# Gate and up of a feed-forward layer: six pairs of k-tiles by seven products instead of three, and the sums of weights on GpSimd instead of VectorE

## The chip, the core and the metric

The kernel runs on one core of a Trainium2 chip. The metric is the device time of one execution in microseconds (us), the median of several runs. Five engines work side by side, each on its own queue of instructions, in the order of that queue: TensorE (PE in the rows, with PEld for its weight loads), VectorE (DVE), ScalarE (ACT), GpSimd (POOL) and SyncE (SP, which here only issues the loads from HBM). An instruction that needs another engine's result waits on a semaphore, and everything behind it on its own queue waits with it.

## The reference

Two transformer blocks over 256 tokens of width 2048, in float32. The change touches the last part of the second block, the feed-forward layer with 5632 hidden columns:

```python
h = rmsnorm(x, ffn_norm_w[l])
x = x + (jax.nn.silu(h @ w_gate[l]) * (h @ w_up[l])) @ w_down[l]
```

`w_gate` and `w_up` are 2048 x 5632 and `w_down` is 5632 x 2048. Everything before this (projections, two recurrences, attention) stays as it is.

## The kernel before

All weights stream from HBM. A piece of weights is one tile of 128 partitions x 1024 float32 (`wr`, 5 buffers), loaded by SP. Since TensorE is fed with a shorter format than float32, each piece is cut in two (`cut`, lines 295 to 315): ScalarE casts it to `wh` (line 312), VectorE subtracts that from the piece and writes the rest to `wl` (line 314). `wh` and `wl` have 5 buffers each. A product of one k-tile is then three matmuls, high by high, high by low and low by high (line 219).

The hidden columns of gate and up are taken in 11 blocks of 512. Blocks 0 to 3, 4 to 7 and 8 to 10 make three parts, and behind each part comes its share of the product with `w_down`. In a block the 16 k-tiles of 128 go in 8 pairs. The tokens are two tiles of 128 (t = 0 and 1), so a pair is two blocks of a 2 x 2 product for gate and two for up. There are two plans for a pair (class `Pair`):

- the plain plan, pieces X (gate) and Y (up): eight products, 24 matmuls of 128x512;
- the plan by seven products, pieces A, E, B and C, a form of Winograd's algorithm: 21 matmuls. It needs sums of weights: `w3` (two halves, lines 305 and 306) and `w4` (two halves, lines 307 and 308), each half one subtraction of 128x512 by VectorE. `w3` takes a `wr` buffer and `w4` one of the 23 general pages (`pg`). A (the gate pair, 1024 wide), E (half of the up pair, 512 wide), B (`w3`, 1024) and C (`w4`, 1024) are then cut as other pieces are. It also needs sums of the activations, made once in `operand3` (names `s1` to `s4`, line 1420 on) and kept in a page for each pair; a plain pair needs a difference (`d`) instead.

`SPAIRS = (1, 3, 5)` says which pairs go by seven products. Three of the seven accumulators are in the PSUM pool of the side work (`ps`), and `ff_mid` (lines 1469 to 1476) empties them behind the last such pair. `ff_done` (line 1478 on) empties the others behind the block, computes silu by tanh, multiplies gate by up, transposes and splits the result for `w_down`.

The order on each queue is made by a scheduler that works from the program's order: loads are asked for 5 pieces ahead (`AHEAD`), pieces are cut up to 4 ahead of their products (`CUT`), and side work (`ff_done` of the block before, for one) is put between.

Of the kernel before, what the change touches and what calls it, by code (L numbers as in the profile page):

```python
# [12 lines left out]
F32R = mybir.dt.float32r  # L13
AF = mybir.ActivationFunctionType
ALU = mybir.AluOpType
# [4 lines left out]
P = 128  # L20
# [7 lines left out]
CV = 2  # L28
# [3 lines left out]
CUT = 4  # L32
WB = 5
AHEAD = 5
SPAIRS = (1, 3, 5)
PARTS = ((0, 4), (4, 8), (8, 11))
WN = 1024
WU = 14
# [119 lines left out]
def kernel(ctx, tc, a, out, dbg=None):  # L158
    nc = tc.nc
    PE, V, A, G, SP = nc.tensor, nc.vector, nc.scalar, nc.gpsimd, nc.sync  # L160
# [3 lines left out]
    pg = ctx.enter_context(tc.tile_pool(name="pg", bufs=PGB))  # L164
# [10 lines left out]
    def nm(s):  # L175
        uid[0] += 1
        return f"{s}{uid[0]}"

    def page(dt=F32, n=1024):
        return pg.tile([P, 1088], dt, tag="pg", name=nm("pg"))[:, :n]  # L180

    def half():
        return hp_.tile([P, 512], F32, tag="hp", name=nm("hp"))
# [4 lines left out]
    def bank():  # L188
        return ps.tile([P, 512], F32, tag="sp", name=nm("sp"))
# [4 lines left out]
    def v3(t, b):  # L194
        return t.rearrange("p (a b) -> p a b", b=b)
# [19 lines left out]
    def act(o, x, f, **kw):  # L215
        return A.activation(out=o, in_=x, func=f, **kw)  # L216
# [18 lines left out]
    def tr(o, x):  # L235
        n = x.shape[0]
        PE.transpose(o, x, ident[:n, :n])  # L237
# [18 lines left out]
    def add(ch):  # L256
        ci = len(chunks)
        chunks.append(ch)
        if ch.kind == "pair":
            pieces.extend((ch, k, n, c) for k, n, c in ch.parts)  # L260
            return ci
        m = -(-ch.nk // ch.per)
        k = 0
        sizes = [(ch.nk * (i + 1)) // m - (ch.nk * i) // m for i in range(m)]
        if ci == 0:
            sizes = FIRST
        for n in sizes:
            pieces.append((ch, k, n, None))
            k += n
        return ci  # L270
# [24 lines left out]
    def cut(i):  # L295
        if i >= len(pieces) or i in split:
            return
        ch, k, n, part = pieces[i]
        w = raw.pop(i)
        if part == "A":  # L300

            w2 = raw[i + 1]
            w3 = raw[i + 2] = wp.tile([P, WN], F32, tag="wr", name=nm("wr"), bufs=RB)
            w4 = raw[i + 3] = page()
            V.tensor_tensor(out=w3[:, :512], in0=w2[:, :512], in1=w[:, :512], op=ALU.subtract)  # L305
            V.tensor_tensor(out=w3[:, 512:], in0=w2[:, :512], in1=w2[:, 512:], op=ALU.subtract)  # L306
            V.tensor_tensor(out=w4[:, :512], in0=w2[:, 512:], in1=w3[:, :512], op=ALU.subtract)
            V.tensor_tensor(out=w4[:, 512:], in0=w[:, 512:], in1=w4[:, :512], op=ALU.subtract)  # L308
        x = w[:, 512:] if part == "E" else w[:, :n * ch.width if part is None else 1024]
        sz = x.shape[1]  # L310
        h = wp.tile([P, WN], F32R, tag="wh", name=nm("wh"), bufs=WB)
        A.copy(out=h[:, :sz], in_=x)  # L312
        l = wp.tile([P, WN], F32R, tag="wl", name=nm("wl"), bufs=WB)
        V.tensor_tensor(out=l[:, :sz], in0=x, in1=h[:, :sz].bitcast(F32), op=ALU.subtract)  # L314
        split[i] = (v3(h[:, :sz], ch.width), v3(l[:, :sz], ch.width))
# [70 lines left out]
    def run_stream():  # L386
# [4 lines left out]
        while i < len(pieces):  # L391
# [5 lines left out]
            for j in range(CUT):  # L397
                cut(i + j)
# [68 lines left out]
    def vec(row):  # L467
        return vt[:, row:row + 1]
# [931 lines left out]
    dform = []  # L1400

    def operand3(nat, n, hi, lo):

        f = v3(page(), S)
        for j in (0, 2):
            b = bank()
            b3 = v3(b, S)
            for q in range(2):
                for t in range(2):
                    tr(b3[:, q, t * P:(t + 1) * P], nat[:, t, (j + q) * P:(j + q + 1) * P])  # L1410
            yield
            for q in range(2):
                act(f[:, j + q, :], b3[:, q, :], AF.Copy, scale=vec(V_FN + 4 * n + j + q))
            k = slice(4 * n + j, 4 * n + j + 2)
            A.copy(out=hi[:, k, :], in_=f[:, j:j + 2, :])
            V.tensor_tensor(out=lo[:, k, :], in0=f[:, j:j + 2, :], in1=hi[:, k, :].bitcast(F32), op=ALU.subtract)
            yield
            p = 2 * n + j // 2
            x = half()
            if p in SPAIRS:  # L1420
                a11, a21, a12, a22 = (f[:, j + q, t * P:(t + 1) * P] for q in range(2) for t in range(2))
                s1, s3, s2, s4 = (x[:, q * P:(q + 1) * P] for q in range(4))
                V.tensor_tensor(out=s1, in0=a21, in1=a22, op=ALU.add)
                V.tensor_tensor(out=s3, in0=a21, in1=a11, op=ALU.subtract)
                V.tensor_tensor(out=s2, in0=s1, in1=a11, op=ALU.subtract)
                V.tensor_tensor(out=s4, in0=a12, in1=s2, op=ALU.subtract)
                h, w, c = page(F32R), 512, 0
                names = [(nme, 2 * p) for nme in ("s1", "s3", "s2", "s4")]
            else:
                V.tensor_tensor(out=v3(x[:, :S], P), in0=f[:, j:j + 2, 0:P], in1=f[:, j:j + 2, P:S], op=ALU.subtract)  # L1430
                if not dform or dform[-1][1] == 512:
                    dform.append([pg.tile([P, 1024], F32R, tag="cv", name=nm("cv"), bufs=CV) if len(dform) < CV else page(F32R), 0])
                h, c = dform[-1]
                w = S
                dform[-1][1] += S
                names = [("d", 2 * p), ("d", 2 * p + 1)]
            A.copy(out=h[:, c:c + w], in_=x[:, :w])
            V.tensor_tensor(out=h[:, 512 + c:512 + c + w], in0=x[:, :w], in1=h[:, c:c + w].bitcast(F32), op=ALU.subtract)
            for q, nme in enumerate(names):
                op3.forms[nme] = (h[:, c + q * P:c + (q + 1) * P], h[:, 512 + c + q * P:512 + c + (q + 1) * P])  # L1440
            for q in range(2):
                op3.t[4 * n + j + q] = (hi, lo, 4 * n + j + q)
                op3.cols[4 * n + j + q] = 1
            yield
# [24 lines left out]
    def ff_mid(po, st):  # L1469

        x, v = page(), page()
        A.copy(out=x[:, :512], in_=po["1"])
        V.tensor_tensor(out=x[:, 512:], in0=x[:, :512], in1=po["6"], op=ALU.add)
        V.tensor_tensor(out=v[:, :512], in0=x[:, 512:], in1=po["7"], op=ALU.add)
        st["x"], st["v"] = x, v
        yield

    def ff_done(po, st, part, k0):

        x, v = st["x"], st["v"]  # L1480
        lo_, hi_ = slice(0, 512), slice(512, 1024)
        g = page()
        V.tensor_tensor(out=g[:, lo_], in0=x[:, lo_], in1=po["2"], op=ALU.add)  # L1483
        V.tensor_tensor(out=g[:, hi_], in0=v[:, lo_], in1=po["4"], op=ALU.add)
        V.tensor_tensor(out=v[:, hi_], in0=x[:, hi_], in1=po["5"], op=ALU.add)
        V.tensor_tensor(out=v[:, lo_], in0=v[:, lo_], in1=po["5"], op=ALU.add)
        V.tensor_tensor(out=v[:, hi_], in0=v[:, hi_], in1=po["3"], op=ALU.add)
        for t, c in ((0, lo_), (1, hi_)):
            act(x[:, c], g[:, c], AF.Tanh, scale=r3h[:, t:t + 1])
        yield  # L1490
        stt(g, x, 1.0, g, ALU.add, ALU.mult)
        mul(g[:, lo_], g[:, lo_], v[:, hi_])
        mul(g[:, hi_], g[:, hi_], v[:, lo_])
        yield
        u = v3(g, 512)
        hi, lo = page(F32R), page(F32R)
        for j in (0, 2):
            b = bank()
            b3 = v3(b, S)
            for q in range(2):  # L1500
                for t in range(2):
                    tr(b3[:, q, t * P:(t + 1) * P], u[:, t, (j + q) * P:(j + q + 1) * P])
            yield
            c = slice(j * S, (j + 2) * S)
            A.copy(out=hi[:, c], in_=b)
            V.tensor_tensor(out=lo[:, c], in0=b, in1=hi[:, c].bitcast(F32), op=ALU.subtract)
            for q in range(j, j + 2):
                opf[part].t[k0 + q] = (v3(hi, S), v3(lo, S), q)
                opf[part].cols[k0 + q] = 1
            yield  # L1510
# [39 lines left out]
    w2 = a["w_in_2"].rearrange("o k n -> (o k) n")  # L1550
# [56 lines left out]
    for n in range(4):  # L1607
        st = {}
        c = slice(n * 512, (n + 1) * 512)
# [22 lines left out]
    for part, (b0, b1) in enumerate(PARTS):  # L1632
        for blk in range(b0, b1):
            st = {}
            c = slice(blk * 512, (blk + 1) * 512)
            add(Pair(wg[:, c], wu[:, c], 16, op3, SPAIRS, lambda po, st=st: ff_mid(po, st),
                     lambda po, st=st, part=part, blk=blk: ff_done(po, st, part, 4 * blk)))
# [28 lines left out]
```

## Time and profile before

| | us |
|---|---|
| median of 3 runs | 2319.6 |
| lowest, highest | 2319.56, 2323.78 |
| the profiled execution, whole | 2321.56 |
| its span in the trace | 2319.7 |
| TensorE busy | 2302.9 (99%) |
| VectorE busy | 1594.3 (69%) |
| ScalarE busy | 1155.2 (50%) |
| GpSimd busy | 91.3 (4%) |

The span is the time from the first to the last instruction of the profiled execution. Busy time is the time in which an engine had an instruction under way; consecutive instructions of one engine overlap a little, so the distance between two starts is shorter than a duration. The feed-forward layer runs from about 1580 us to the end.

### The profile page before, as it was taken

The page shows a single profiled execution, that of the slowest core. Times are in us where ns is not written, and L with a number is a line of the kernel's source. Part 1 is how long each engine was busy: PE and PEld are TensorE (multiplying, and loading weights), DVE is VectorE, ACT ScalarE, POOL GpSimd, SP SyncE. Part 2 cuts the span into 40 slices and gives each one's busy share as a digit, 9 for nine tenths or more (in the row PEclk, how much of TensorE's full clock was granted, in tenths as well). Part 3 has the DMA queues.
Part 4 walks back from the last instruction along what each step waited for, and adds up shares of the span by engine and source line. Part 5 has one row for each costly group of instructions (what it writes and reads, how often), then busy time and mean ns, then how long its engine had stood idle before and what let it go on. Part 6 is the DMA issues. An engine that isn't in the chain of part 4 may idle for free.

```text
span 2319.7 us, 29508 instructions
## 1 busy us (share of the span) xinstructions
PE 2302.9 (99%) x11101; PEld 1899.4 (82%) x11101; DVE 1594.3 (69%) x2164; ACT 1155.2 (50%) x1521; POOL 91.3 (4%) x122
## 2 busy tenths in 40 slices
PE   8999999999999999999999999999999999999998
PEld 7888888888888888888888777888878888888886
DVE  6777678785676655455555566667897588856985
ACT  5553444544454444444444455456555355544553
POOL 0112001000100000000010000000000000000000
PEclk9999999999999999999999999999999999999999
DMA  7667545666555666666676554455657556665664
GB/s 245 184 182 211 167 137 173 178 203 183 168 163 158 187 185 196 203 201 203 187 211 182 162 148 140 145 185 161 222 176 227 175 184 203 222 196 170 204 217 137
DMA packets 225198, 427.97 MB, mean 184 GB/s; under 512 B 20200, under 2 KB 20624, under 8 KB 225056
## 3 DMA queue, kind: packets, MB, share of 16 engines
q1 hardware_dynamic: 219136, 411.08, 58.2%
q0 software_dynamic: 5056, 13.70, 2.1%
q8 instruction: 87, 1.43, 0.3%
q10 hardware_dynamic: 864, 1.31, 0.2%
q14 instruction: 55, 0.45, 0.1%
HBM read 422.31 MB, written 3.73 MB: 184 GB/s over the span
## 4 chain that ended last, share of the span: by engine, by line
PE 97%; DMA 1%; DVE 1%; issue 0%; ACT 0%; SPq 0%; POOLq 0%; POOL 0%; DVEq 0%; ACTq 0%
PE mm L219 89%; PE sp L219 4%; PE sp L237 3%; DMA wr<-in_w_up_dram 1%; PE sp L797 1%; PE sp L1227 0%; DMA wr<-in_w_in_dram 0%; DVE wl L314 0%; ACT wh L312 0%; SPq L248 0%; SPq L288 0%; DVE wr L306 0%; DVE wr L305 0%; ACT pg L216 0%; DVE pg L1483 0%
## 5 line engine op out<-in xcount | busy, mean ns | idle before, releaser
L219 PE MATMUL mm<-wh,hl 128*128 128x512 f32 x4186 | 1337.3, 394 | 2.4 <-ACT wh L312 1.4
L314 DVE TENSOR_TENSOR wl<-wr,wh 128x1024 fp32r<-128x1024 f32 (+2 forms) x811 | 966.5, 1200 | 518.3 <-ACT wh L312 514.9
L312 ACT CAST wh<-wr 128x1024 fp32r<-128x1024 f32 (+2 forms) x811 | 831.5, 1033 | 893.8 <-PE mm L219 806.5
L219 PEld LDWEIGHTS mm<-wh,hl 128*128 128x128 f32 x4186 | 784.0, 188 | 168.6 <-issue 5.8
L219 PE MATMUL mm<-wl,hl 128*128 128x512 f32 x2093 | 819.3, 392 | 0.6 <-DVE wl L314 0.6
L219 PE MATMUL mm<-wh,pg 128*128 128x512 f32 x1780 | 565.2, 391 | 0.0
L219 PEld LDWEIGHTS mm<-wl,hl 128*128 128x128 f32 x2093 | 393.7, 188 | 80.9 <-DVE wl L314 1.8
L219 PEld LDWEIGHTS mm<-wh,pg 128*128 128x128 f32 x1780 | 333.7, 188 | 69.7 <-issue 0.9
L219 PE MATMUL mm<-wl,pg 128*128 128x512 f32 x890 | 346.6, 389 | 0.0
L219 PEld LDWEIGHTS mm<-wl,pg 128*128 128x128 f32 x890 | 167.1, 188 | 34.4
L237 PE MATMUL sp<-con,pg 128*128 128x128 f32 x555 | 85.8, 275 | 5.2 <-DMA pg<-in_consts_dram 4.9
L237 PEld LDWEIGHTS sp<-con,pg 128*128 128x128 f32 x555 | 68.1, 141 | 21.8 <-issue 7.0
L312 ACT CAST wh<-pg 128x1024 fp32r<-128x1024 f32 x33 | 34.7, 1053 | 82.6 <-DVE pg L308 54.6
L213 DVE SCALAR_TENSOR_TENSOR pg<-cv,vt,pg 128x255 f32<-128x255 f32 (+2 forms) x144 | 61.6, 478 | 1.3 <-ACT pg L216 1.2
L219 PE MATMUL mm<-wh,cv 128*128 128x512 f32 x176 | 61.5, 390 | 0.0
L314 DVE TENSOR_TENSOR wl<-pg,wh 128x1024 fp32r<-128x1024 f32 x33 | 40.4, 1224 | 22.8 <-ACT wh L312 22.8
L219 PE MATMUL sp<-pg,pg 128*128 128x128 f32 (+3 forms) x320 | 50.2, 315 | 0.0
L219 PEld LDWEIGHTS sp<-pg,pg 128*128 128x128 f32 (+1 forms) x320 | 42.8, 190 | 6.1 <-issue 2.9
L216 ACT ACTIVATE pg<-sp,vt 128x256 fp32r<-128x256 f32 (+1 forms) x64 | 28.4, 471 | 28.5 <-PE sp L237 17.2
L219 PEld LDWEIGHTS mm<-wh,cv 128*128 128x128 f32 x176 | 33.0, 188 | 6.7
L216 ACT ACTIVATE pg<-pg 128x512 f32<-128x512 f32 (+2 forms) x54 | 35.3, 674 | 6.2 <-DVE pg L890 3.1
L305 DVE TENSOR_TENSOR wr<-wr,wr 128x512 f32<-128x512 f32 x33 | 22.8, 691 | 21.5 <-DMA wr<-in_w_up_dram 21.4
(273 smaller groups left out, 1190.3 us busy)
## 6 DMA issues: line engine op xcount, KB each, us to landing
wr<-in_w_in_dram SPq DMA_DIRECT2D x416, 512.0 KB, 3.8
wr<-in_w_out_dram SPq DMA_DIRECT2D x96, 512.0 KB, 4.5
wr<-in_w_gate_dram SPq DMA_DIRECT2D x88, 512.0 KB, 3.9
wr<-in_w_up_dram SPq DMA_DIRECT2D x88, 512.0 KB, 4.6
wr<-in_w_down_dram SPq DMA_DIRECT2D x88, 512.0 KB, 4.7
pg<-zsc POOLq DMA_DIRECT2D x8, 384.0 KB, 4.6
pg<-in_x_dram SPq DMA_DIRECT2D x4, 512.0 KB, 6.0
pg<-gsc POOLq DMA_DIRECT2D x4, 512.0 KB, 6.3
```

Of the source, the lines that this page charges most:

```text
L213: return V.scalar_tensor_tensor(out=o, in0=x, scalar=s, in1=y, op0=op0, op1=op1)
L216: return A.activation(out=o, in_=x, func=f, **kw)
L219: PE.matmul(o, l, r, start=start, stop=stop)
L237: PE.transpose(o, x, ident[:n, :n])
L305: V.tensor_tensor(out=w3[:, :512], in0=w2[:, :512], in1=w[:, :512], op=ALU.subtract)
L312: A.copy(out=h[:, :sz], in_=x)
L314: V.tensor_tensor(out=l[:, :sz], in0=x, in1=h[:, :sz].bitcast(F32), op=ALU.subtract)
L797: PE.matmul(o, l, r_, start=True, stop=True, tile_position=(row, col))
```

## The change

Pairs 1 to 6 of the eight go by seven products, where pairs 1, 3 and 5 did. The four subtractions that make `w3` and `w4` are issued to GpSimd (`G`) instead of VectorE (`V`), for all of these pairs. The page for the first pair's sums of activations now comes from the small pool `cv`, which the second page of differences had before.

```diff
-SPAIRS = (1, 3, 5)
+SPAIRS = (1, 2, 3, 4, 5, 6)
...
-            V.tensor_tensor(out=w3[:, :512], in0=w2[:, :512], in1=w[:, :512], op=ALU.subtract)
-            V.tensor_tensor(out=w3[:, 512:], in0=w2[:, :512], in1=w2[:, 512:], op=ALU.subtract)
-            V.tensor_tensor(out=w4[:, :512], in0=w2[:, 512:], in1=w3[:, :512], op=ALU.subtract)
-            V.tensor_tensor(out=w4[:, 512:], in0=w[:, 512:], in1=w4[:, :512], op=ALU.subtract)
+            G.tensor_tensor(out=w3[:, :512], in0=w2[:, :512], in1=w[:, :512], op=ALU.subtract)
+            G.tensor_tensor(out=w3[:, 512:], in0=w2[:, :512], in1=w2[:, 512:], op=ALU.subtract)
+            G.tensor_tensor(out=w4[:, :512], in0=w2[:, 512:], in1=w3[:, :512], op=ALU.subtract)
+            G.tensor_tensor(out=w4[:, 512:], in0=w[:, 512:], in1=w4[:, :512], op=ALU.subtract)
...
-                h, w, c = page(F32R), 512, 0
+                if p == SPAIRS[0]:
+                    h = pg.tile([P, 1024], F32R, tag="cv", name=nm("cv"), bufs=CV)
+                else:
+                    h = page(F32R)
+                w, c = 512, 0
...
-                    dform.append([pg.tile([P, 1024], F32R, tag="cv", name=nm("cv"), bufs=CV) if len(dform) < CV else page(F32R), 0])
+                    dform.append([pg.tile([P, 1024], F32R, tag="cv", name=nm("cv"), bufs=CV) if len(dform) < CV - 1 else page(F32R), 0])
```

On VectorE, within a block of the first part, this stood before, from the cut of one pair's C to the next plain pair (`wl<-pg` is a C, 128x512 of `wl` an E):

```order
L314 TENSOR_TENSOR wl_13863<-wr_13829,wh_13861 128x1024
L314 TENSOR_TENSOR wl_13872<-wr_13847,wh_13870 128x1024
L305 TENSOR_TENSOR wr_13880<-wr_13868,wr_13859 128x512
L306 TENSOR_TENSOR wr_13880<-wr_13868 128x512
L314 TENSOR_TENSOR wl_13888<-wr_13859,wh_13886 128x1024
L314 TENSOR_TENSOR wl_13898<-wr_13868,wh_13896 128x512
L1506 TENSOR_TENSOR pg_13746<-sp_13806,pg_13745 128x512
L307 TENSOR_TENSOR pg_13881<-wr_13868,wr_13880 128x512
L314 TENSOR_TENSOR wl_13916<-wr_13880,wh_13914 128x1024
L308 TENSOR_TENSOR pg_13881<-wr_13859,pg_13881 128x512
L314 TENSOR_TENSOR wl_13934<-pg_13881,wh_13932 128x1024
```

In the changed kernel VectorE's queue in the middle of a block is this:

```order
L314 TENSOR_TENSOR wl_13907<-wr_13868,wh_13905 128x1024
L314 TENSOR_TENSOR wl_13914<-wr_13885,wh_13912 128x512
L1510 TENSOR_TENSOR pg_13822<-sp_13880,pg_13821 128x512
L314 TENSOR_TENSOR wl_13926<-wr_13899,wh_13924 128x1024
L314 TENSOR_TENSOR wl_13938<-pg_13900,wh_13936 128x1024
L314 TENSOR_TENSOR wl_13954<-wr_13922,wh_13952 128x1024
L314 TENSOR_TENSOR wl_13961<-wr_13934,wh_13959 128x512
L314 TENSOR_TENSOR wl_13973<-wr_13946,wh_13971 128x1024
L314 TENSOR_TENSOR wl_13985<-pg_13947,wh_13983 128x1024
```

The two plain pieces and the four sums are gone from between: A, E, B and C of one pair follow on those of the pair before.

On GpSimd the stretch from the first part's start to the end of the layer held one small power for the normalisation and the four loads of `final_norm_w_2`. Now two pairs in the middle of a block look so:

```order
L305 TENSOR_TENSOR wr_13600<-wr_13588,wr_13576 128x512
L306 TENSOR_TENSOR wr_13600<-wr_13588 128x512
L307 TENSOR_TENSOR pg_13601<-wr_13588,wr_13600 128x512
L308 TENSOR_TENSOR pg_13601<-wr_13576,pg_13601 128x512
L305 TENSOR_TENSOR wr_13647<-wr_13635,wr_13623 128x512
L306 TENSOR_TENSOR wr_13647<-wr_13635 128x512
L307 TENSOR_TENSOR pg_13648<-wr_13635,wr_13647 128x512
L308 TENSOR_TENSOR pg_13648<-wr_13623,pg_13648 128x512
```

The sums stand there pair behind pair, 24 in each block and 264 in all, and the four loads of `final_norm_w_2` stand behind the last of them.

## Rows read from the trace of the kernel before

**Rows 1.** The page's first part: busy us (share of the span) xinstructions of each engine.

```profile
PE 2302.9 (99%) x11101; PEld 1899.4 (82%) x11101; DVE 1594.3 (69%) x2164; ACT 1155.2 (50%) x1521; POOL 91.3 (4%) x122
```

**Rows 2.** Two whole blocks: length, busy us (xinstructions) of PE, PEld, DVE, ACT, POOL, clock, DMA.

```profile
1951.46:1994.71 43.25, 43.25 (x196) 35.50 (x194) 39.09 (x48) 24.43 (x28) 0.00 (x0) 1.00 0.62 195
1909.07:1951.46 42.39, 42.39 (x191) 34.90 (x191) 38.86 (x47) 23.57 (x28) 0.00 (x0) 1.00 0.62 198
```

**Rows 3.** The chain that ended last, two pieces in blocks: start us, us, what.

```profile
1921.12 31.90 PE mm L219 x140
...
2222.35 32.00 PE mm L219 x141
```

**Rows 4.** VectorE's groups from 1580 to 2300 us: xcount | busy us, mean ns | idle before.

```profile
L314 DVE TENSOR_TENSOR wl<-pg,wh 128x1024 fp32r<-128x1024 f32 x33 | 40.4, 1224 | 22.8 <-ACT wh L312 22.8
...
L204 DVE TENSOR_TENSOR pg<-pg,pg 128x512 f32<-128x512 f32 x22 | 14.2, 688 | 0.0
L213 DVE SCALAR_TENSOR_TENSOR pg<-pg,pg 128x1024 f32<-128x1024 f32 x11 | 13.5, 1223 | 0.0
```

**Rows 5.** VectorE in order of time, within blocks: start us, us, line, operation.

```profile
1642.09 0.69 DVE L314 TENSOR_TENSOR wl<-wr,wh 128x512 fp32r<-128x512 f32 x1
...
1964.68 0.68 DVE L305 TENSOR_TENSOR wr<-wr,wr 128x512 f32<-128x512 f32 x1
1965.28 0.69 DVE L306 TENSOR_TENSOR wr<-wr 128x512 f32<-128x512 f32 x1
...
1968.82 1.22 DVE L314 TENSOR_TENSOR wl<-wr,wh 128x1024 fp32r<-128x1024 f32 x1
1969.95 0.69 DVE L308 TENSOR_TENSOR pg<-wr,pg 128x512 f32<-128x512 f32 x1
```

**Rows 6.** ScalarE's casts from 1580 to 2300 us, the two shapes apart.

```profile
L312 ACT CAST wh<-wr 128x1024 fp32r<-128x1024 f32 x267 | 276.7, 1053 | 229.4 <-PE mm L219 205.5 <-issue 10.2 <-DMA wr<-in_w_down_dram 8.3
...
L312 ACT CAST wh<-wr 128x512 fp32r<-128x512 f32 x33 | 20.5, 620 | 17.4 <-PE mm L219 16.9 <-DMA wr<-in_w_up_dram 0.5
```

**Rows 7.** GpSimd in order of time: seven of its small powers, over the whole span.

```profile
34.88 0.72 POOL L241 TENSOR_TENSOR rstd<-ms,mhalf 128x2 f32<-128x2 f32 x1 [32.55 <-DVE ms L210]
...
113.92 1.66 POOL L241 TENSOR_TENSOR rr<-n,mhalf 128x8 f32<-128x8 f32 x1 [0.40 <-DVE n L207]
...
680.95 2.97 POOL L241 TENSOR_TENSOR f<-so,mhalf 128x8 f32<-128x8 f32 x1 [20.03 <-DVE so L210]
...
785.00 1.66 POOL L241 TENSOR_TENSOR f<-so,mhalf 128x8 f32<-128x8 f32 x1 [2.77 <-DVE so L210]
...
1189.46 1.75 POOL L241 TENSOR_TENSOR rf<-ms,mhalf 128x2 f32<-128x2 f32 x1 [24.34 <-DVE ms L210]
1191.88 0.69 POOL L241 TENSOR_TENSOR p<-ms,mhalf 128x2 f32<-128x2 f32 x1 [0.67 <-DVE ms L210]
...
1604.84 1.60 POOL L241 TENSOR_TENSOR r<-ms,mhalf 128x2 f32<-128x2 f32 x1 [96.60 <-DVE ms L210]
```

**Rows 8.** VectorE in order of time, beside five of those powers.

```profile
114.66 0.69 DVE L204 TENSOR_TENSOR pg<-sp,pg 128x512 f32<-128x512 f32 x1 [0.83 <-PE sp L219]
...
681.17 1.22 DVE L314 TENSOR_TENSOR wl<-wr,wh 128x1024 fp32r<-128x1024 f32 x1
...
785.27 1.23 DVE L314 TENSOR_TENSOR wl<-wr,wh 128x1024 fp32r<-128x1024 f32 x1 [0.36 <-ACT wh L312]
...
1189.41 1.23 DVE L314 TENSOR_TENSOR wl<-wr,wh 128x1024 fp32r<-128x1024 f32 x1
...
1604.67 1.22 DVE L314 TENSOR_TENSOR wl<-pg,wh 128x1024 fp32r<-128x1024 f32 x1
```

**Rows 9.** GpSimd's wide operations, which write only, grouped by line.

```profile
L781 POOL MEMSET pg<- 128x1024 f32 x4 | 3.8, 970 | 0.0
...
L784 POOL MEMSET hp<- 128x512 f32 x4 | 2.0, 523 | 81.3 <-PE sp L219 63.2 <-DVE pg L213 17.9 <-POOLq L1653 0.3
```

**Rows 10.** The last 10 us, columns as in rows 2.

```profile
2310.00:2320.00 10.00, 1.05 (x5) 0.55 (x3) 2.21 (x5) 2.06 (x4) 0.55 (x1) 0.67 0.55 204
```

## The prediction, made before the changed kernel ran

> **What bounds the kernel now.** I read the page's shares first: TensorE is busy 99% of the span, VectorE 69%, GpSimd 4% [rows 1]. A share over the whole span hides its stages, so I next cut out whole feed-forward blocks, from one silu product of ff_done to the next. Two neighbouring blocks take 42.39 and 43.25 us, 42.8 on average. TensorE never stops in them, but VectorE is busy for 39 of the 43 us, ScalarE for 24, GpSimd not at all [rows 2]. The chain that ended last says the same: long runs of matmuls, 140 in 31.90 us and 141 in 32.00, with nothing between [rows 3], which is 0.228 us from matmul to matmul. A block has 3 x 21 + 5 x 24 = 183 of them, or 41.7 us, and the transposes of ff_done make up the rest. So TensorE sets the time, and VectorE would be next, with about 4 us to spare in a block.
>
> **The change part by part.**
>
> *Matmuls removed.* Three more pairs in each of 11 blocks, three matmuls less each: 99 x 0.228 = 22.6 us, all of it on the path. A block would need 174 matmuls, 39.7 us, and with 0.8 us of transposes TensorE's floor is 40.5 us. A pair by seven products takes it 21 x 0.228 = 4.8 us, a plain one 5.5.
>
> *Cuts added.* A pair by seven products has 3.5 pieces to cut where a plain one has 2. VectorE starts the next operation 1.13 us behind a start of 1024 columns and 0.60 behind one of 512 [rows 5], so a pair's cuts take it 3 x 1.13 + 0.60 = 4.0 us. For ScalarE they are 3 x 1.05 + 0.62 = 3.8 us a pair [rows 6]. Both are below 4.8 us: alone, neither would bind.
>
> *Sums removed from VectorE.* 33 pairs with four subtractions at a pitch of 0.60 us. Its own work in a block goes from 3 x (2.4 + 4.0) + 10 x 1.13 = 30.5 us to 6 x 4.0 + 4 x 1.13 = 28.5, beside some 8 us for ff_mid and ff_done. By that alone it is relieved.
>
> *Sums added on GpSimd.* 66 pairs with four, 264 in all. No wide two-input operation of GpSimd is in the trace. The nearest rows are its memsets: 0.523 us for 512 columns and 0.970 for 1024 [rows 9], so one stream of 512 takes 0.45 us on a start of 0.08. A subtraction reads two streams and writes one. If all three run side by side it takes 0.52; if all follow each other, 3 x 0.45 + 0.08 = 1.42. I take 1.1, nearer to the upper end: two reads behind each other, 0.98, and a start nearer to the 0.7 us that even two columns cost [rows 7] than to a memset's. Four of them are 4.4 us, and just fit beside TensorE's 4.8.
>
> The Trainium skill, "GPSIMD Engine Reference", section 3.1, has such a price: about 2.6 cycles an element for a two-input operation, since its two reads share one port. That would be an estimate of 1.12 us for 512 columns; no row here shows it, and the sum below would be some 5 us more.
>
> *The two engines against each other.* This term decides. GpSimd's powers of two columns take 0.72 and 0.69 us at 34.88 and 1191.88, but 1.75 and 1.60 us at 1189.46 and 1604.84 [rows 7]. In the two long cases VectorE had just begun a cut, a subtraction with both inputs in SBUF: at 1189.41 until 1190.64, and at 1604.67 until 1605.89 [rows 8]. The powers end at 1191.21 and 1606.44, that is 0.57 and 0.55 us behind VectorE's end. So GpSimd waited for the whole of VectorE's operation and then needed its own time less 0.15 us. The one of eight columns at 680.95 shows it again: 2.97 instead of 1.66 us, with a cut at 681.17 that ends at 682.39. Long idle time ahead is no other cause: the power at 34.88 had waited 32.55 us before it and was short.
>
> Nearly all that VectorE does in these pairs is of that kind (both inputs of line 314 are in SBUF), and the 264 sums read SBUF too. Whatever the two do, they do in turn. For a pair: VectorE's cuts at full duration, since nothing overlaps their start where the engines alternate, 3 x 1.22 + 0.69 = 4.35 us [rows 4, 5]; GpSimd's sums 4 x (1.1 - 0.15) = 3.8 us. Together 8.15 us, where TensorE needs 4.8.
>
> For a block: 6 x 8.15 = 48.9, the four pieces of the plain pairs 4 x 1.13 = 4.5, and the three two-input operations of ff_done that read only SBUF, 1.22 + 2 x 0.65 = 2.5 [rows 4]: 55.9 us. The other eight or so of ff_mid and ff_done take one input from PSUM; I put them at nothing, since the power at 113.92 ran its usual 1.66 us beside such a one at 114.66 [rows 7, 8]. If they too had to take turns, they would add 8 x 0.69 = 5.5 us a block. From TensorE's side it comes out alike: two plain pairs at its own pace, 10.9 us, in which the cuts of the next pair run ahead as far as five buffers allow, then five pairs at 8.15 and the last at 4.8 make 56.5. Against 42.8 us the 55.9 are 13.1 us more, and 11 blocks make 144 us. The 22.6 us saved are inside this difference; they are not seen, because TensorE waits.
>
> The Trainium skill, "SBUF — State Buffer", section "Who interferes with whom", has the rule: VectorE and GpSimd share a port pair, a VectorE instruction with two SBUF inputs contends with a GpSimd one that reads SBUF, and whichever comes first holds it for the whole instruction. The rows agree for GpSimd behind VectorE; but the cut at 785.27 took its usual 1.23 us inside a power that ran from 785.00 to 786.66 [rows 7, 8], so here GpSimd did not hold anything for a whole instruction. By the rule to the letter a pair would cost 4 x 1.1 + 4.35 = 8.75 us, a block 59.5, and the kernel 2503 us.
>
> *The rest.* operand3 makes the sums of activations for three more pairs, a few small VectorE operations once, around 1600 us: some 3 us of work under TensorE's matmuls, and 3 us if that cover were gone. One more page of the 23 is held by them, and w4 takes a page for 66 pairs instead of 33; I put no price on it. On GpSimd's queue the four loads of final_norm_w_2 now stand behind the last sum, ahead of w_down's last share, which uses them.
>
> *The sum.* 2321.6 us for the profiled execution + 144 = 2465.6. It was 2.0 us above the median of the runs, so I forecast 2464 us.
>
> **The rivals.**
>
> *VectorE doesn't wait for GpSimd.* The trace shows only the other direction, and the cut at 785.27 is for it. Then only a sum waits: on average half a cut, 0.6 us, in about two of three cases, so 1.5 us a sum, 6.0 a pair and, from TensorE's side, 10.9 + 5 x 6.0 + 4.8 = 45.7 us a block: 2.9 more than before, in all 32, 2352 us. Against it: reads of 512 columns last far longer than those of eight, so a cut should now meet them. With sums of 1.0 us it is 2330, with 1.42 it is 2420.
>
> *The sums are short, or don't meet the cuts: faster.* In-turn work costs less than before if 6x + 7.0 is below 42.8 us, so at x = 5.97 us a pair, which is (5.97 - 4.35) / 4 = 0.40 us behind a cut or 0.55 alone. That is the lower end of the price of a sum, where the three streams run side by side. Without any contention the saving is whole: 2319.6 - 22.6 = 2297 us. Against it stand the three long powers; for it, only that no wide sum has been seen. With a sum near 0.55 the time is as before.
>
> *TensorE's clock falls.* With TensorE waiting for a quarter of the layer, the granted clock could go from 2.4 to 1.2 GHz, as the 0.67 of the last 10 us shows it does where TensorE is nearly idle [rows 10]. Its floor would be 174 x 0.456 + 1.6 = 81 us a block, 2740 us if it lasted. Against it: the waits are a microsecond or two each, with matmuls between.
>
> **How the numbers follow.** The engines in turn, both ways: 0.63. VectorE not waiting: 0.20. Short sums or no contention: 0.10 faster, and 0.03 within 0.2%, which is about what a measurement of this kernel can tell from no change. A lower clock: 0.04. The forecast's own ends are sums of 0.98 us (a pair 7.67, 2432 us) and of 1.42 us (a pair 9.43, 2550 us). The range takes in the first rival down to 2330, so 2330 to 2550; it leaves out the faster cases, the clock and a little above. Faster 0.10, same 0.03, slower 0.87.
>
> **What would show it.** In the changed profile the blocks should be about 56 us long, with TensorE near 72% busy in them and GpSimd over half. If I am right, a sum ends close to 1 us behind the end of a cut, cuts stretch beyond 1.22 us or start late while a sum runs, and TensorE waits for line 314 and for casts of w3 and w4. Cuts at 1.22 us throughout with sums at 1.5 us would be the first rival; sums at 1.1 us or less beside running cuts, the second. A granted clock below 1.00 in the blocks would be the third.

## The result, and the profile after

The changed kernel takes 2493.7 us (median of 4 runs, 2492.3 to 2497.0) against 2320.4 before: 1.0746 times as long, 95% interval 1.0727 to 1.0765, or 173 us more. The forecast was 2464 us in a range of 2330 to 2550. The engines on the changed kernel's page (busy us, share of the span, instructions):

```profile
PE 2353.9 (94%) x11002; PEld 1884.7 (76%) x11002; DVE 1810.9 (73%) x2107; ACT 1205.3 (48%) x1587; POOL 611.9 (25%) x386
```

And the shares of its chain of waits:

```profile
PE 74%; POOL 13%; DVE 6%; issue 4%; DMA 2%; ACT 1%; SPq 0%; POOLq 0%; DVEq 0%; ACTq 0%
```

The 99 matmuls are gone (11101 to 11002, compare [rows 1]), yet the span grew. VectorE lost 57 instructions and is busy 217 us longer. GpSimd went from 91 to 612 us, and it has entered the chain, with 13% of the span. Now five whole blocks, cut as in [rows 2] (length, then busy us of PE, PEld, DVE, ACT and POOL, clock, DMA):

```profile
1666.66:1724.47 57.81, 48.10 (x186) 34.94 (x185) 57.13 (x40) 29.05 (x34) 46.16 (x24) 0.94 0.44 142
1724.47:1783.61 59.14, 47.21 (x184) 33.21 (x183) 58.59 (x40) 28.60 (x34) 47.38 (x25) 0.97 0.45 143
1988.05:2043.50 55.45, 44.51 (x172) 32.38 (x171) 54.85 (x41) 28.08 (x33) 44.59 (x23) 0.94 0.41 133
2043.50:2103.97 60.47, 48.30 (x191) 33.28 (x190) 58.69 (x40) 28.86 (x34) 48.57 (x26) 1.00 0.45 143
2305.74:2362.36 56.62, 45.43 (x172) 32.19 (x171) 56.03 (x40) 28.09 (x33) 46.18 (x24) 0.94 0.41 138
```

They take 57.9 us on average, where two blocks of before took 42.8. VectorE is busy for 97 to 99% of it, with fewer instructions than before (40 for 47). Inside a block the rows in order of time show why (start us, us, engine, line, operation). GpSimd's:

```profile
1682.42 2.27 POOL L305 TENSOR_TENSOR wr<-wr,wr 128x512 f32<-128x512 f32 x1
1684.65 2.26 POOL L306 TENSOR_TENSOR wr<-wr 128x512 f32<-128x512 f32 x1
1686.88 2.26 POOL L307 TENSOR_TENSOR pg<-wr,wr 128x512 f32<-128x512 f32 x1
1689.22 1.60 POOL L308 TENSOR_TENSOR pg<-wr,pg 128x512 f32<-128x512 f32 x1
1690.79 2.26 POOL L305 TENSOR_TENSOR wr<-wr,wr 128x512 f32<-128x512 f32 x1
```

VectorE's in the same microseconds (x3 is three instructions in one row):

```profile
1683.57 2.20 DVE L314 TENSOR_TENSOR wl<-pg,wh 128x1024 fp32r<-128x1024 f32 x1
1685.69 6.21 DVE L314 TENSOR_TENSOR wl<-wr,wh 128x1024 fp32r<-128x1024 f32 x3
```

A cut that took 1.22 us [rows 4, 5] takes 2.20, and a sum 2.26. Both engines have an instruction under way all the time, and each instruction contains the wait for the other. From the first sum of one pair to that of the next it is 1690.79 - 1682.42 = 8.37 us, which is also the median of such distances within the blocks; the forecast was 8.15. The fourth sum meets E's cut of 512 columns and is the shorter for it.

VectorE's other operations show what meets a sum and what doesn't. Two of its groups from 1580 to 2480 us, the first with both inputs in SBUF, the second with one of them in PSUM (`sp`):

```profile
L204 DVE TENSOR_TENSOR pg<-pg,pg 128x512 f32<-128x512 f32 x22 | 31.0, 1450 | 0.3
L1510 DVE TENSOR_TENSOR pg<-sp,pg 128x512 fp32r<-128x512 f32 x22 | 14.7, 680 | 0.4 <-ACT pg L1509 0.4
```

The first took 688 ns before [rows 4] and takes 1450 now. The second, and a block's seven additions of ff_mid and ff_done with a PSUM input, took 0.68 to 0.69 us before and take 0.68.

The times of ff_done's silu products in all 11 blocks account for the whole difference. Measured from one of them to the next, where a block follows another in its part it is 14.8 us longer on average (five blocks), where it is a part's last 19.7, 18.5 and 22.3, and where it is the first of a part, with what stands ahead of it, 16.9, 12.9 and 10.9. That is 175 us, as the spans say (2495.0 against 2319.7); from the last one to the end both kernels need 71 us.

### The profile page after: what moved, and what is told of

Same layout as the page of the kernel before. It is cut to its first block, busy times and chain, and to the rows that moved or that the text cites. A ratio compares the mean times of both kernels' runs of the same rounds, so it can differ in the third digit from the quotient of the medians.

```text
span 2495.0 us, 29833 instructions
## 1 busy us (share of the span) xinstructions
PE 2353.9 (94%) x11002; PEld 1884.7 (76%) x11002; DVE 1810.9 (73%) x2107; ACT 1205.3 (48%) x1587; POOL 611.9 (25%) x386
## 4 chain that ended last, share of the span: by engine, by line
PE 74%; POOL 13%; DVE 6%; issue 4%; DMA 2%; ACT 1%; SPq 0%; POOLq 0%; DVEq 0%; ACTq 0%
PE mm L219 67%; DVE wl L314 4%; POOL wr L306 4%; PE sp L219 4%; POOL wr L305 4%; POOL pg L307 3%; POOL pg L308 2%; PE sp L237 2%; DMA wr<-in_w_up_dram 2%; ACT wh L312 1%; PE sp L797 1%; DVE pg L204 0%; PE sp L1227 0%; DVE pg L213 0%; DMA wr<-in_w_down_dram 0%
## 5 line engine op out<-in xcount | busy, mean ns | idle before, releaser
L314 DVE TENSOR_TENSOR wl<-wr,wh 128x1024 fp32r<-128x1024 f32 (+2 forms) x844 | 1138.8, 1361 | 520.5 <-ACT wh L312 517.3
L219 PE MATMUL mm<-wh,hl 128*128 128x512 f32 x3988 | 1291.1, 397 | 21.5 <-DVE pg L1487 20.2
L219 PE MATMUL mm<-wh,pg 128*128 128x512 f32 x1912 | 623.1, 396 | 3.3 <-DVE pg L1487 3.2
L219 PE MATMUL mm<-wl,pg 128*128 128x512 f32 x956 | 390.8, 409 | 68.5 <-DVE wl L314 63.9
L305 POOL TENSOR_TENSOR wr<-wr,wr 128x512 f32<-128x512 f32 x66 | 137.1, 2078 | 369.5 <-DMA wr<-in_w_up_dram 300.5
L306 POOL TENSOR_TENSOR wr<-wr 128x512 f32<-128x512 f32 x66 | 138.3, 2095 | 0.0
L314 DVE TENSOR_TENSOR wl<-pg,wh 128x1024 fp32r<-128x1024 f32 x66 | 133.9, 2028 | 2.7 <-ACT wh L312 1.7
L307 POOL TENSOR_TENSOR pg<-wr,wr 128x512 f32<-128x512 f32 x66 | 134.8, 2043 | 0.0
L312 ACT CAST wh<-pg 128x1024 fp32r<-128x1024 f32 x66 | 69.1, 1047 | 134.6 <-POOL pg L308 119.3
L308 POOL TENSOR_TENSOR pg<-wr,pg 128x512 f32<-128x512 f32 x66 | 117.4, 1778 | 5.2
```

The costliest lines, as they stand in the source:

```text
L219: PE.matmul(o, l, r, start=start, stop=stop)
L305: G.tensor_tensor(out=w3[:, :512], in0=w2[:, :512], in1=w[:, :512], op=ALU.subtract)
L306: G.tensor_tensor(out=w3[:, 512:], in0=w2[:, :512], in1=w2[:, 512:], op=ALU.subtract)
L307: G.tensor_tensor(out=w4[:, :512], in0=w2[:, 512:], in1=w3[:, :512], op=ALU.subtract)
L308: G.tensor_tensor(out=w4[:, 512:], in0=w[:, 512:], in1=w4[:, :512], op=ALU.subtract)
```

## The experiments

The theory is the prediction's: a GpSimd operation that reads SBUF and a VectorE operation with two inputs from SBUF take turns. Against it stand the extra pairs themselves (buffers, order, loads), GpSimd's chain of four sums as such, and waits at the block ends. The times of before measured beside these runs were 2320.8 to 2321.2 us. Edits are against the changed kernel. The four kernels in the table without an interval leave out sums that the reference needs, and ran once each, so a few microseconds among them say nothing.

| run | us | ratio to before (95%) |
|---|---|---|
| changed kernel | 2493.7 | 1.0746 (1.0727 to 1.0765) |
| six_early | 2487.1 | 1.0715 (1.0697 to 1.0733) |
| six_on_vector | 2430.1 | 1.0470 (1.0455 to 1.0486) |
| four_one_gpsimd | 2392.3 | 1.0304 (1.0290 to 1.0318) |
| two_sums | 2387.0 | one run |
| one_input | 2381.2 | one run |
| four_spread | 2372.6 | 1.0225 (1.0210 to 1.0241) |
| four_on_vector | 2352.9 | 1.0148 (1.0131 to 1.0164) |
| four_early | 2340.9 | 1.0084 (1.0069 to 1.0099) |
| three_on_gpsimd | 2333.9 | 1.0054 (1.0038 to 1.0071) |
| write_only | 2301.7 | one run |
| no_sums | 2297.3 | one run |

### What the matmuls are worth: no_sums

```diff
-            w3 = raw[i + 2] = wp.tile([P, WN], F32, tag="wr", name=nm("wr"), bufs=RB)
-            w4 = raw[i + 3] = page()
-            G.tensor_tensor(...)
...
+            raw[i + 2], raw[i + 3] = w2, w
```

> Six pairs without any sums of weights: B is cut from the up piece and C from the gate piece (the sums are left out of the computation). It shows what 99 matmuls less are worth when nothing takes turns: VectorE's cuts 28.5 us a block and 8 of ff_mid and ff_done lie under TensorE's 40.5. Theory: about 2300 us, 20 below before, TensorE 99% busy in the blocks. Rival (six pairs are bound elsewhere even so: ff_mid later, PSUM, loads): 2320 us or more.

It took 2297.3 us, 23.7 less than before; the price of 99 matmuls was 22.6. Two of its blocks:

```profile
1646.57:1686.98 40.41, 40.41 (x183) 33.38 (x182) 37.39 (x41) 28.80 (x33) 0.00 (x0) 1.00 0.66 211
1686.98:1727.39 40.41, 40.41 (x183) 33.41 (x182) 37.37 (x41) 28.79 (x33) 0.00 (x0) 1.00 0.67 209
```

TensorE's floor had been put at 40.5 us a block. So six pairs in themselves, with their loads, casts and cuts and ff_mid one pair later, do not stand in the way; the sums do, with the buffers that they take (a `wr` for `w3` and a page for `w4` are gone here too). The next run has the `wr` back and is nearly as fast, and two_sums below is slow without the page, so the buffers are not it.

### Wide GpSimd work that reads nothing: write_only

```diff
-            w4 = raw[i + 3] = page()
-            G.tensor_tensor(...)
...
+            raw[i + 3] = w3
+            for _ in range(4):
+                G.memset(w3, 0.0)
```

> Six pairs; in place of each pair's four sums GpSimd writes w3 four times (memset of 1024 columns, some 0.97 us each, 3.9 us a pair), reads nothing, and C is cut from w3 too (the sums are left out of the computation). Theory (the turns are over reading SBUF): GpSimd is about as busy, but no cut stretches beyond 1.23 us, TensorE binds again and the kernel takes about 2300 us. Rival (any wide GpSimd work beside VectorE, or the extra step through GpSimd's queue, costs the time): 2400 us or more, with cuts near 2 us.

2301.7 us. A block of it:

```profile
1685.95:1726.41 40.46, 40.46 (x184) 33.32 (x183) 37.32 (x42) 29.02 (x33) 22.99 (x24) 1.00 0.70 208
```

The groups of the memsets and of the cuts from 1580 to 2280 us (line 306 is the memset, line 312 the cut):

```profile
L306 POOL MEMSET wr<- 128x1024 f32 x264 | 252.6, 957 | 446.0 <-DVE wl L312 434.6
...
L312 DVE TENSOR_TENSOR wl<-wr,wh 128x1024 fp32r<-128x1024 f32 (+1 forms) x399 | 442.6, 1134 | 144.3 <-ACT wh L310 136.9
```

264 wide operations stand on GpSimd's queue, 23 us a block, in the place of the sums, B and C wait for them, and next to nothing is lost (4.4 us against no_sums): no cut took longer than 1.23 us. So GpSimd's load and the step through its queue are not the cause. Four sums undisturbed would be longer than four memsets, 24 x 1.28 = 31 us a block, but that too is below TensorE's 40.5. What is left is that the sums read.

### GpSimd operations with one input: one_input

```diff
-            G.tensor_tensor(out=w3[:, :512], in0=w2[:, :512], in1=w[:, :512], op=ALU.subtract)
+            G.tensor_copy(out=w3[:, :512], in_=w2[:, :512])
...
-            G.tensor_tensor(out=w4[:, 512:], in0=w[:, 512:], in1=w4[:, :512], op=ALU.subtract)
+            G.tensor_copy(out=w4[:, 512:], in_=w[:, 512:])
```

> Six pairs; each of the four sums on GpSimd is replaced by a copy of one 512-column SBUF tile (the subtractions are left out). Theory (turns over reading SBUF): a copy also reads SBUF and waits for a cut, but alone it is shorter than a sum's 1.28 us, near 0.6; a pair costs 3.97 + 4 x 0.5 = 6 us, the kernel about 2345 us. Rival (only operations with two inputs meet): cuts stay at 1.22 us and it takes about 2300 us.

It took 2381.2 us. GpSimd's copies at two places, in order of time:

```profile
1717.40 1.61 POOL L306 COPY wr<-wr 128x512 f32<-128x512 f32 x1
1718.95 1.60 POOL L307 COPY pg<-wr 128x512 f32<-128x512 f32 x1
...
1729.60 0.61 POOL L307 COPY pg<-wr 128x512 f32<-128x512 f32 x1
1730.15 0.61 POOL L308 COPY pg<-wr 128x512 f32<-128x512 f32 x1
```

VectorE's cuts there:

```profile
1718.45 1.63 DVE L314 TENSOR_TENSOR wl<-pg,wh 128x1024 fp32r<-128x1024 f32 x1
...
1731.32 1.23 DVE L314 TENSOR_TENSOR wl<-pg,wh 128x1024 fp32r<-128x1024 f32 x1 [2.71 <-ACT wh L312]
```

A copy takes 0.61 us where no cut runs, and 1.60 beside one; the cut then takes 1.63 instead of 1.23. So one input of GpSimd's is enough to meet the cuts, and the rival of that expectation falls. The size was off by 36 us: GpSimd's copies wait 232 us for loads of the gate piece (179 of them in two waits between the parts, but the rest within them), and TensorE waits 29 us for casts, which the sum of turns does not contain. Why the loads came late there was not followed up.

### Two sums instead of four: two_sums

```diff
-            w4 = raw[i + 3] = page()
+            raw[i + 3] = w3
...
-            G.tensor_tensor(out=w4[:, :512], in0=w2[:, 512:], in1=w3[:, :512], op=ALU.subtract)
-            G.tensor_tensor(out=w4[:, 512:], in0=w[:, 512:], in1=w4[:, :512], op=ALU.subtract)
```

> Six pairs, only the two sums of w3 on GpSimd; the two of w4 are left out and C is cut from w3. Theory (turns): a pair costs 3.97 + 2 x 1.10 = 6.2 us, a block 6 x 6.2 + 7 + 2 for the boundary = 46 us, the kernel about 2355 us; a sum still takes 2.2 us beside a cut. Rival (what binds is GpSimd's own chain of four dependent sums, not the turns): two sums of 1.3 us fit well beside TensorE's 4.8 us, and it takes about 2300 us.

2387.0 us: the rival of a chain of four sums falls, since two of them still cost 66 us against before. The turns are the expected ones. This row is VectorE's run of eight cuts, two pairs (the cut is line 312 here):

```profile
1671.84 12.46 DVE L312 TENSOR_TENSOR wl<-wr,wh 128x1024 fp32r<-128x1024 f32 x8
```

12.46 / 2 = 6.23 us a pair, where 6.2 were expected. But between such runs VectorE idles half a microsecond for a cast, and a block that follows another takes 47 to 49 us instead of 46. In-turn work alone is a lower bound: the kernel came out 32 us above the 2355 expected.

### The two parts of the change apart: six_on_vector and three_on_gpsimd

The first is the changed kernel with `V.` for `G.` in the four sums.

> One part of the change alone: six pairs by seven products, but the sums stay on VectorE. Theory (the two engines take turns at SBUF): no sum meets a cut any more, so cuts go back to 1.13 us apart and a pair costs VectorE 4.0 + 4 x 0.60 = 6.4 us instead of 8.37 for the two engines; a block is 6 x 6.4 + 4.5 + 8.2 = 51 us, 8 more than before, and the kernel about 2410 us: slower than before, faster than the changed kernel by some 80 us. Rival (the extra pairs themselves, by buffers, pages or the order, cost the time, and the engine doesn't matter): 2480 us or more.

2430.1 us. A block:

```profile
1656.60:1710.53 53.93, 45.81 (x183) 33.39 (x182) 51.12 (x64) 28.45 (x34) 0.00 (x0) 0.97 0.48 156
```

VectorE's queue, in order of time:

```profile
1678.25 0.68 DVE L308 TENSOR_TENSOR pg<-wr,pg 128x512 f32<-128x512 f32 x1
1678.85 0.68 DVE L305 TENSOR_TENSOR wr<-wr,wr 128x512 f32<-128x512 f32 x1
1679.45 0.68 DVE L306 TENSOR_TENSOR wr<-wr 128x512 f32<-128x512 f32 x1
1680.06 0.68 DVE L307 TENSOR_TENSOR pg<-wr,wr 128x512 f32<-128x512 f32 x1
1680.66 1.21 DVE L314 TENSOR_TENSOR wl<-pg,wh 128x1024 fp32r<-128x1024 f32 x1
```

VectorE's work is the 51 us expected, and no cut takes longer than 1.23 us, but VectorE is not kept full: the block takes 54, and the kernel 20 us more than the 2410 expected. Even so this is 64 us faster than with the sums on GpSimd: on VectorE a sum takes 0.60 us from the start of one to the start of the next, and on GpSimd it takes 1.10 us out of the two engines' common time.

The second is the changed kernel with `SPAIRS = (1, 3, 5)`.

> The other part alone: three pairs as before, their sums on GpSimd. Theory (turns): a pair by seven products costs the two engines 8.37 us, the plain pair behind it 2.3, together 10.6 where TensorE needs 10.3; a block stays near TensorE's 42.8 us, so 2320 to 2345 us, with cuts of 2.1 to 2.3 us wherever a sum runs. Rival (moving the sums only relieves VectorE): 2320 us or a little below, with cuts of 1.22 us throughout.

2333.9 us, 0.5% (13 us) slower than before with the same matmuls. A block of it:

```profile
1652.15:1696.11 43.96, 43.64 (x196) 35.65 (x196) 40.41 (x35) 24.07 (x27) 22.08 (x12) 1.00 0.57 184
```

Two cuts one after the other, the first beside the end of a sum (the longest cut in this run took 2.34 us):

```profile
1706.36 1.71 DVE L314 TENSOR_TENSOR wl<-wr,wh 128x1024 fp32r<-128x1024 f32 x1
1708.10 1.23 DVE L314 TENSOR_TENSOR wl<-pg,wh 128x1024 fp32r<-128x1024 f32 x1
```

Twelve sums fewer on VectorE's queue, and it is busy 1.4 us longer in this block than the 39.0 us that the blocks of [rows 2] have on average. With a plain pair between, 10.6 us of turns in two pairs nearly fit TensorE's 10.3, as expected, so little shows in the time. Six pairs in a row leave no such room. Apart, the two parts of the change cost 109 and 13 us; together 173.

### The block ends: six_early

At nine block ends of the changed kernel TensorE waits for ff_done's reads of PSUM, since they stand behind cuts that a sum stretches. TensorE at one of them (in brackets the wait ahead of the instruction and what ended it):

```profile
1775.65 0.39 PE L219 MATMUL mm<-wh,cv 128*128 128x512 f32 x1
1779.11 0.47 PE L219 MATMUL mm<-wh,hl 128*128 128x512 f32 x1 [3.08 <-DVE pg L1487]
```

VectorE there:

```profile
1774.88 2.89 DVE L314 TENSOR_TENSOR wl<-wr,wh 128x1024 fp32r<-128x1024 f32 x2
1777.69 0.68 DVE L1489 TENSOR_TENSOR pg<-pg,mm 128x512 f32<-128x512 f32 x1
1778.29 0.68 DVE L1487 TENSOR_TENSOR pg<-pg,mm 128x512 f32<-128x512 f32 x1
```

```diff
-SPAIRS = (1, 2, 3, 4, 5, 6)
+SPAIRS = (0, 1, 2, 3, 4, 5)
```

> The changed kernel with pairs 0 to 5 instead of 1 to 6, sums on GpSimd: the same work, with two plain pairs at a block's end in place of one at each end. In the changed kernel TensorE waits some 3 us at nine of the block ends for ff_done's reads of PSUM, which stand behind stretched cuts on VectorE. If these waits are why a block takes 2 us more than the turns alone make it (57.9 against 55.9), ending the seven-product pairs earlier takes them away: about 2470 us. If the turns are the whole of it (a pair measures 8.37 us, six of them 50.2), the time stays within 10 us of the changed kernel's 2494.

The waits for line 1487 (23.3 us in the changed kernel) are gone, and the time falls by 6.6 us, to 2487.1. Blocks still take 59.0 and 58.5 us; what is gained lies in the last blocks of the parts, which take 54.3 to 55.8 instead of 57.6 to 61.8. So these waits are mostly time that the turns would have taken anyway, and the turns are nearly the whole of it.

### Versions that might beat both: four pairs

VectorE has about 4 us to spare in a block of before, so a fourth pair was tried, with the sums on VectorE (`V.` in all four lines, three placements) and with one pair's sums on GpSimd. This is four_on_vector's placement:

```diff
-SPAIRS = (1, 2, 3, 4, 5, 6)
+SPAIRS = (1, 3, 4, 6)
```

> Four pairs (1, 3, 4, 6) by seven products, all sums on VectorE. VectorE's work in a block: 4 x 6.4 + 8 x 1.13 + 8.2 = 42.8 us against TensorE's 42.1. If VectorE can be kept that full, 2312 us, 0.3% below before; if the two neighbouring pairs 3 and 4 stall TensorE, 2320 to 2335 us.

In four_one_gpsimd the sums of pair 4 stay on GpSimd:

```diff
+            Q = G if k // 2 == 4 else V
-            G.tensor_tensor(out=w3[:, :512], in0=w2[:, :512], in1=w[:, :512], op=ALU.subtract)
+            Q.tensor_tensor(out=w3[:, :512], in0=w2[:, :512], in1=w[:, :512], op=ALU.subtract)
...
```

> Four pairs (1, 3, 4, 6), the sums of pair 4 on GpSimd, those of the other three on VectorE. VectorE has 40.4 us of work in a block and waits for up to 4 x 1.1 = 4.4 us of sums, some of it beside its reads of PSUM. Theory (turns): 2315 to 2330 us, no better than the four pairs on VectorE. Rival (one pair's sums on GpSimd find enough idle time): 2312 us, TensorE's floor for four pairs.

> Four pairs (0, 2, 4, 6), never two in a row, all sums on VectorE. VectorE's own work is 42.8 us a block against TensorE's 42.1, as in the run with pairs 1, 3, 4 and 6, which took 2353 us with 3 us waits at block ends. If the even spread lets VectorE stay full, 2315 us; if ff_done behind pair 6 stalls TensorE again, about 2350.

> Four pairs (0, 2, 3, 5), all sums on VectorE: as the run with pairs 1, 3, 4 and 6, but the last one is pair 5 as before, so that ff_done's reads meet no sums of the same block. If the late last pair causes the waits at block ends, they go and the kernel takes 2315 to 2325 us; if VectorE's 42.8 us of work in a block are too much however they lie, 2345 or more.

All four are slower than before: 2352.9, 2392.3, 2372.6 and 2340.9 us. One block of each, first four_on_vector:

```profile
1700.38:1746.02 45.64, 42.14 (x183) 34.33 (x183) 42.94 (x53) 24.99 (x29) 0.00 (x0) 0.96 0.57 185
```

four_one_gpsimd:

```profile
1705.32:1754.56 49.24, 44.32 (x184) 35.22 (x184) 43.37 (x49) 25.18 (x29) 7.20 (x4) 0.93 0.56 171
```

four_spread:

```profile
1709.82:1757.65 47.83, 43.41 (x181) 33.73 (x180) 41.87 (x52) 25.15 (x29) 0.00 (x0) 0.96 0.56 170
```

four_early:

```profile
1699.05:1744.44 45.39, 43.84 (x190) 34.21 (x189) 42.92 (x53) 24.86 (x29) 0.00 (x0) 1.00 0.61 186
```

VectorE has the 43 us of work that was worked out, and the block takes 2.5 us and more above it: a queue in fixed order, with casts and loads to wait for, was not kept full at any placement. With the last pair at 5 the waits for line 1487 go (26.2 us in four_on_vector, 0.3 in four_early), and the run is the best of the four, but it ended near the slow one of its two expectations. The other three came out slower than either of theirs, four_one_gpsimd by 62 us. Moving the sums of one pair in each block to GpSimd added 39 us to four_on_vector; by the turns alone it would be 4 x (1.10 - 0.60) = 2.0 us a block, 22 in all, and the rest is not explained. Its sums were not free, at least. Three pairs on VectorE, the kernel before, is the fastest of the versions here that compute all of the reference.

## Why the prediction was right

*The bound and the saving.* TensorE bound the blocks, and 99 matmuls were worth 22.6 us: no_sums gave 23.7. Right.

*Cuts and casts added.* VectorE's 28.5 + 8 us a block were to lie under TensorE's 40.5: 37.4 busy in no_sums, at 40.41 us a block. Right.

*The turns.* This was the deciding term, read off three long powers on GpSimd in [rows 7] and the cuts beside them in [rows 8]. write_only, one_input and the stretched rows of the changed kernel bear it out, in both directions. The first rival, in which VectorE does not wait, falls: cuts of 2.20 us were not there before. The one row that had spoken for it, a cut of 1.23 us inside a power of eight columns, differs in length: that power reads eight columns, a sum 512. That the length decides is likely, but no run here has lengths between.

*The size of the terms.* A sum alone was put at 1.1 us. The groups of GpSimd in the changed kernel hold the shortest of each line at 1.27 to 1.29 us, within the bounds of 0.98 to 1.42. In the turns it was put at 0.95 and takes (8.37 - 3 x 1.13 - 0.60) / 4 = 1.10. A cut was put at its full 1.22 us in the turns, since nothing should overlap its start; in fact its pitch of 1.13 holds there, for 1.10 + 1.13 is the distance of 2.23 between sums. The two errors go against each other: 8.37 us for a pair, not 8.15. Six of them and the same 4.5 and 2.5 us for the rest make 57.2 us a block, where 57.9 was measured and 55.9 forecast. That the price of a pair came so near owes something to luck, as the two errors (0.6 us too little for the sums, 0.36 too much for the cuts) partly cancel. TensorE was to be busy 72% of a block and is 81%, and GpSimd, at over half, is 80%.

*Operations with an input from PSUM.* They were put at nothing in the turns, and the rows above bear that out: 0.68 us, as before.

*What the sum left out.* The forecast took all 11 blocks alike, at 13.1 us more each, and fell short by 31 us of the 175. The five blocks that follow another make up 9 of these 31, the first ones of the parts 1, and the last ones, 18.5 to 22.3 us longer, 21. Those last blocks took 39 us before, not the 42.8 that the forecast subtracts, which is 11 of their 21 us; the other 10 are that they now take 57.6 to 61.8 us and not 55.9. In six_early they take 54.3 to 55.8, so these 10 hang on where the six pairs lie in the block. More about them was not tried.

*GpSimd's price on a page.* The Trainium skill, "GPSIMD Engine Reference", section 3.1, led to an estimate of 1.12 us; the trace has 1.27 to 1.29 for a sum undisturbed.

*The rule of the shared port.* The Trainium skill, "SBUF — State Buffer", section "Who interferes with whom", also says that a VectorE instruction with two SBUF inputs meets a GpSimd one that reads SBUF and not one that only writes it. write_only (cuts of 1.23 us at most beside memsets) and one_input (1.63 us beside copies) agree. That the holder keeps it for the whole instruction had given 8.75 us a pair; the trace has 8.37, the difference being that a cut counts there with its pitch of 1.13 us and not with 1.22.

*The other rivals.* Short sums: no, they are 1.28 us, far from the break-even of 0.55. The clock: it did fall in places, as the granted clock of one pair of the changed kernel shows beside its neighbour's:

```profile
1682.42:1690.79 8.37, 5.96 (x21) 3.63 (x21) 8.34 (x5) 3.57 (x4) 8.29 (x6) 1.00 0.37 125
1690.79:1699.14 8.35, 6.87 (x21) 4.92 (x21) 8.32 (x5) 3.56 (x4) 8.27 (x5) 0.80 0.39 128
```

At 0.80 on average, which is 1.2 GHz for part of that stretch, the pair took the same 8.35 us: TensorE was waiting anyway. Nor do the five blocks follow the clock: the longest, 60.47 us, has 1.00, and the shortest, 55.45, has 0.94. So the sign that had been named for this rival is there, and no time was seen to hang on it.

## What to carry to other kernels

Before work moves from VectorE to GpSimd, ask whether both read SBUF: here a GpSimd operation with SBUF inputs and a VectorE one with two of them added up instead of running side by side, and GpSimd was the slower of the two (1.28 against 0.69 us for a subtraction of 512 columns). An engine that is 4% busy is then no free place; the sum of both engines' work in the stage is what must fit under the bound. A few short operations of the idle engine, compared with and without the neighbour's work beside them, showed one direction of this before anything was built.

## What the runs showed of the hardware

Busy time does not tell work from waiting here: VectorE's 55 to 59 us a block in the changed kernel contain 17 to 21 us of waiting inside its instructions (no_sums has 37.4 us without them, for the same work), with hardly any idle time recorded ahead of them. Nor are two inputs needed to be held up: two VectorE operations of the changed kernel that read one tensor of 128x2 in SBUF (line 210 at 1604.70 us, line 207 at 1606.57) took 1.06 and 1.26 us beside sums, and 0.17 in the kernel before. A copy of 512 columns on GpSimd takes 0.61 us undisturbed and a two-input subtraction 1.28. TensorE's granted clock fell to 0.91 on average over 100 us in six_early (1600 to 1700 us) and to 0.95 in the changed kernel, where its longest wait for a cut is 2.7 us; in the changed kernel, where TensorE isn't the bound, no time was seen to hang on it.
